# A fused matmul, bias and residual on one core: twelve deferred tiles, other load groups, and a different last-store split

## The chip, the core and the metric

The kernel runs on one core of a Trainium2 chip. The metric is device time in microseconds (us). The engines go by their short names: PE does matrix products and transposes, DVE, ACT and POOL work on elements, and SP issues the transfers (DMAs), which 16 DMA engines carry out. Most of the runs below are timed in rounds, each kernel against the kernel before on the same chip; a ratio is the mean time of one kernel's fast runs over the mean of the other's fast runs of the same rounds, so it is not quite the ratio of the medians that are quoted. The span in a profile is about 1.8 us shorter than the device time.

## The reference

```python
x:        (16, 512, 1024) float32      weight: (1024, 768) float32
bias:     (768,) float32               residual: (16, 512, 768) float32
out = matmul(x, weight) + bias + residual      # float32
```

The kernel moves 87.05 MB and does 64 tiles of 128 rows: input 33.6 MB, residual and output 25.2 MB each, weight 3.1 MB.

## The kernel before

A tile is 128 rows, one on each partition. Sixteen tiles form a stage; partition p holds 16 neighbouring rows of HBM, so a load of j tiles has one run of j rows per partition. SP issues every DMA, in the order of a list. The list has `x` (input), `w`, `b`, `r` (residual), `s` (store), `c` (last pieces of the last tile), each with stage and tiles; a fifth number of a store is the partition at which it is cut in two DMAs.

```python
EARLY_END = 14     # tiles below it are finished without the residual, which POOL adds later
TMP_ROW = 16       # their products wait in these rows of the residual and output buffer R
W_ROW = 14         # where the float32 weights land, in R as well
ADDS = [10, 14, 3, 2, 4, 15, 11, 1, 5, 13, 7, 6, 12, 9, 0, 8]
ORDER = [..., ('r', 2, 6, 16), ('s', 1, 0, 16), ('x', 3, 0, 6), ('r', 3, 0, 7), ('x', 3, 6, 16),
 ('r', 3, 7, 16), ('s', 2, 0, 16), ('s', 3, 0, 10), ('s', 3, 10, 12, 108), ('s', 3, 12, 14),
 ('s', 3, 14, 15), ('c', 3, 15, 0), ('c', 3, 15, 1)]
# ... cut ...
            elif kind == "r":        # when may a residual load be issued
                need = [("store", t - RR) for t in range(J * S + j0, J * S + j1) if t >= RR]
                # ... cut: also after the casts of weights and the adds whose rows it overwrites
# ... cut ...
                edges = [0, *cut, P]
                for p0, p1 in zip(edges, edges[1:]):
                    K_(nc.sync.dma_start(
                        out=out_d[S, p0:p1, j0:j1, n0:n0 + nl],
                        in_=R[p0:p1, (J * S + j0) % RR:(J * S + j0) % RR + j1 - j0, n0:n0 + nl],
                    ))
# ... cut ...
    def finish(t):
        p = PO[t % HEAD]
        if t < EARLY_END:            # product + bias; POOL adds the residual later
            K_(nc.vector.tensor_add(out=tmp(t), in0=p, in1=bias_sb))
        else:                        # POOL has added the bias to the residual already
            K_(nc.vector.tensor_add(out=row(t), in0=p, in1=row(t)))
# ... cut ...
    for t in range(HEAD, n_t):       # the main loop
        cast(t + 2)                  # ACT: float32 input to bfloat16
        pool_adds(t + 1)
        transp(t + 1)                # PE: four transposes, then a DVE copy
        # ... cut: 16 matmuls of tile t
        finish(t - 1)
        # ... cut
```

## Time and profile before

| | kernel before |
|---|---|
| device time, first three runs | 211.26 us median (210.89 to 211.57) |
| span of the profiled run | 209.4 us |
| last DVE add ends | 204.48 us |
| last store lands on its 16 engines | 206.18 to 208.30 us |

The landings come from the semaphore events of the trace: a store over 128 partitions has 16 of them (the last store's run from 206.18 to 208.30), read here as one for each of the 16 DMA engines, at the time when its share has landed. The store of 108 rows has 12 and that of 20 rows 10, beside one just after the issue (194.87 and 196.17) that is not counted. No view numbers the engines. The numbers 0 to 15 that the prediction and the expectations give them are labels by the rows that an engine carries, an estimate from the counts of landings: 108 rows on 12 engines are nine each, 20 on 10 are two; in the changed kernel, 100 on 10 are ten, 28 on 14 are two. The traces agree with it: eight of the ten landings of the 20-row store come 0.45 to 0.48 us after one of the 108-row store (two rows of 0.234 us), and in the changed kernel each of the ten landings of the 100-row store has one of the 28-row store 0.21 to 0.25 us after it (two rows of 0.121 us). That a label means the same engine under both cuts was assumed, not shown.

The views that carry the argument are shown in the prediction.

```profile
101.05 0.60 PE L157 MATMUL pt<-ident,xb 128*128 128x128 f32 x4
104.08 0.60 PE L157 MATMUL pt<-ident,xb 128*128 128x128 f32 x4
107.12 0.60 PE L157 MATMUL pt<-ident,xb 128*128 128x128 f32 x4
```

The middle line is tile 32, the first tile of the third stage.

### The profile page before, as it was taken

Reading aid. Unit: us, or ns where it says so; the run is one execution under the profiler, and the core shown is the slowest. Engines: PE = TensorE matmul, PEld = TensorE weight load, DVE = VectorE, ACT = ScalarE, POOL = GpSimd, SP = SyncE. Lnnn points to the kernel's source line nnn. Section 1 sums busy time; section 2 is a strip of 40 time slices with the busy share of each in tenths; the row PEclk is TensorE's granted clock in tenths of the full one; section 3 lists DMA queues with packets and bytes.
Section 4 is the critical chain, followed back from the end, with each engine's and each line's share of the span. In section 5 each row is a group of like instructions: output and inputs, shape, how many; then the busy total and the mean of one; then the engine's idle time right before and its main releaser. Section 6 shows DMA issues by size and latency. Waiting matters only on the chain.

```text
span 209.4 us, 3113 instructions
## 1 busy us (share of the span) xinstructions
PE 202.3 (97%) x1298; PEld 130.3 (62%) x1298; DVE 104.7 (50%) x140; ACT 66.1 (32%) x69; POOL 115.9 (55%) x72
## 2 busy tenths in 40 slices
PE   7999999999999999999999999999999999999990
PEld 2455666666666666666666666666666666666650
DVE  0448555445544554554455454645544554554460
ACT  2444513312730371310460083320180065330000
POOL 2100039769999806997049603999009940799200
PEclk9999999999999999999999999999999999999998
DMA  6999999999989899899999999999999999998984
GB/s 232 426 425 429 428 433 457 393 464 410 472 378 495 383 494 415 385 415 444 408 435 479 408 417 474 441 412 390 424 476 399 459 407 449 451 441 384 415 354 166
DMA packets 4780, 87.24 MB, mean 417 GB/s; under 512 B 538, under 2 KB 666, under 8 KB 1694
## 3 DMA queue, kind: packets, MB, share of 16 engines
q1 hardware_dynamic: 4766, 87.05, 97.6%
q8 instruction: 10, 0.16, 0.3%
q14 instruction: 4, 0.03, 0.0%
HBM read 61.88 MB, written 25.17 MB: 416 GB/s over the span
## 4 chain that ended last, share of the span: by engine, by line
PE 92%; DMA 4%; ACT 1%; DVE 1%; SPq 0%; issue 0%
PE psum_o L164 78%; PE pt L157 13%; DMA x_tile<-in_x_dram 4%; PE psum_o L258 1%; ACT xb L146 1%; DVE xt L158 0%; DVE ro L262 0%; SPq L119 0%; SPq L122 0%
## 5 line engine op out<-in xcount | busy, mean ns | idle before, releaser
L164 PE MATMUL psum_o<-w_sb,xt 128*128 128x512 bf16 x1008 | 174.0, 326 | 0.3 <-DVE xt L158 0.3
L164 PEld LDWEIGHTS <-xt 128*128 128x128 bf16 x1008 | 98.5, 98 | 59.0 <-DVE xt L158 0.7
L189 POOL TENSOR_TENSOR ro<-ro,bias_sb 128x768 f32<-128x768 f32 x50 | 88.9, 1822 | 48.0 <-DMA ro<-in_residual_dram 37.4
L149 ACT CAST xb<-x_tile 128x1024 bf16<-128x1024 f32 x60 | 59.7, 1043 | 113.8 <-DMA x_tile<-in_x_dram 62.7
L158 DVE COPY xt<-pt 128x1024 bf16<-128x1024 bf16 x64 | 44.0, 691 | 84.9 <-PE pt L157 84.8
L199 DVE TENSOR_TENSOR ro<-psum_o,ro 128x768 f32<-128x768 f32 x49 | 46.5, 948 | 4.3 <-POOL ro L189 3.2
L185 POOL TENSOR_TENSOR ro<-ro 128x768 f32<-128x768 f32 x14 | 25.0, 1815 | 25.1 <-DMA ro<-in_residual_dram 25.0
L157 PE MATMUL pt<-ident,xb 128*128 128x128 f32 x256 | 38.5, 274 | 0.2 <-ACT xb L146 0.2
L157 PEld LDWEIGHTS pt<-ident,xb 128*128 128x128 f32 x256 | 29.9, 142 | 9.0 <-ACT xb L146 1.1
L195 DVE TENSOR_TENSOR ro<-psum_o,bias_sb 128x768 f32<-128x768 f32 x14 | 13.2, 948 | 0.0
L208 PE MATMUL psum_o<-warm 128*128 128x512 bf16 x12 | 5.3, 632 | 1.2 <-DVE warm_a L204 1.2
L229 ACT CAST w_sb<-ro 128x768 bf16<-128x768 f32 x4 | 3.3, 832 | 3.7 <-DMA ro<-in_weight_dram 3.7
L208 PEld LDWEIGHTS <-warm 128*128 128x128 bf16 x12 | 1.6, 144 | 3.9 <-issue 2.8
L229 POOL CAST w_sb<-ro 128x768 bf16<-128x768 f32 x1 | 0.8, 822 | 5.5 <-DMA ro<-in_weight_dram 5.5
L149 DVE CAST xb<-x_tile 128x1024 bf16<-128x1024 f32 x1 | 0.7, 693 | 4.4 <-DMA x_tile<-in_x_dram 4.4
L146 ACT CAST xb<-x_tile 128x512 bf16<-128x512 f32 x3 | 1.8, 616 | 3.4 <-PE psum_o L164 1.7
L258 PE MATMUL psum_o<-w_sb,xt 128*128 128x512 bf16 (+1 forms) x16 | 2.8, 326 | 0.0
L229 DVE CAST w_sb<-ro 128x768 bf16<-128x768 f32 x3 | 1.7, 558 | 2.0 <-DMA ro<-in_weight_dram 2.0
L147 DVE CAST xb<-x_tile 128x512 bf16<-128x512 f32 x3 | 1.2, 424 | 2.4 <-DMA x_tile<-in_x_dram 2.4
L258 PEld LDWEIGHTS <-xt 128*128 128x128 bf16 x16 | 1.6, 98 | 1.1
L223 PE MATMUL psum_o<-warm 128*128 128x512 bf16 x6 | 1.6, 379 | 0.0
L262 DVE TENSOR_TENSOR ro<-psum_o,ro 128x512 f32<-128x512 f32 (+1 forms) x2 | 1.1, 558 | 0.9 <-PE psum_o L258 0.8
(14 smaller groups left out, 5.1 us busy)
## 6 DMA issues: line engine op xcount, KB each, us to landing
out_dram<-ro SPq DMA_DIRECT2D x3, 6144.0 KB, 34.1
x_tile<-in_x_dram SPq DMA_DIRECT2D x3, 5120.0 KB, 24.1
ro<-in_residual_dram SPq DMA_DIRECT2D x3, 3840.0 KB, 25.2
x_tile<-in_x_dram SPq DMA_DIRECT2D x3, 3072.0 KB, 40.2
ro<-in_residual_dram SPq DMA_DIRECT2D x3, 2304.0 KB, 17.5
x_tile<-in_x_dram SPq DMA_DIRECT2D x4, 1024.0 KB, 8.2
x_tile<-in_x_dram SPq DMA_DIRECT2D x2, 2048.0 KB, 21.0
out_dram<-ro SPq DMA_DIRECT2D x1, 3840.0 KB
```

Of the source, the lines that this page charges most:

```text
L146: K_(nc.scalar.copy(out=dst[:, 0:K // 2], in_=src[:, 0:K // 2]))
L149: K_((nc.scalar.copy if how == "s" else nc.vector.tensor_copy)(out=dst, in_=src))
L157: K_(nc.tensor.transpose(out=pt[:, q, :], in_=words[:, ts(q, P)], identity=ident))
L158: K_(nc.vector.tensor_copy(out=XT[t % XT_N].rearrange("p q m e -> p (q m e)"), in_=pt.rearrange("p q m -> p (q m)").bitcast(BF16),))
L164: K_(nc.tensor.matmul(PO[t % HEAD][:, n0:n0 + nl], lhsT=XT[t % XT_N][:, q, :, e], rhs=w_sb[:, q, e, n0:n0 + nl], start=(q == 0 and e == 0) ...
L185: K_(nc.gpsimd.tensor_add(out=r, in0=r, in1=tmp(t)))
L189: K_(nc.gpsimd.tensor_add(out=r, in0=r, in1=bias_sb))
L195: K_(nc.vector.tensor_add(out=tmp(t), in0=p, in1=bias_sb))
L199: K_(nc.vector.tensor_add(out=row(t), in0=p, in1=row(t)))
L208: K_(nc.tensor.matmul(PO[0][:, 0:512], lhsT=warm[:, 0:P], rhs=warm, start=True, stop=True))
L229: K_(copy(out=w_sb[:, q, e, :], in_=w_st[:, 2 * q + e, :]))
L258: K_(nc.tensor.matmul(p, lhsT=XT[t % XT_N][:, q, :, e], rhs=w_sb[:, q, e, n0:n0 + nl], start=(q == 0 and e == 0), stop=(q == n_q - 1 and e ...
```

## The change

Its intent: defer fewer tiles (12, not 14), load the first nine residual tiles at once, regroup the loads of the third stage (the first input load holds eleven tiles in place of six, the first residual load ten) and the stores of the first, and split the last stores differently. In place of tiles 58 and 59 (108 rows on 12 engines, 20 on 10), tile 55 is held back and stored as 100 rows on 10 engines and 28 on 14, to take work from the engines that are late at the end. The whole diff:

```diff
--- before.py
+++ after.py
@@ -18,10 +18,10 @@
 XT_N = 4
 XB_N = 4
 WARM = 12
-EARLY_END = 14
-TMP_ROW = 16
-W_ROW = 14
-ADDS = [10, 14, 3, 2, 4, 15, 11, 1, 5, 13, 7, 6, 12, 9, 0, 8]
+EARLY_END = 12
+TMP_ROW = 18
+W_ROW = 5
+ADDS = [6, 14, 3, 4, 8, 1, 15, 2, 5, 9, 13, 12, 11, 7, 0, 10]
 HEAD_ORDER = [('cast', 0, 'v'), ('cast', 1, 's'), ('tr', 0), ('tr', 1), ('wc', 0, 0, 's'), ('wc', 0, 1, 'g'),
  ('warm', 3), ('mm', 0, 0), ('mm', 1, 0), ('cast', 2, 'sv'), ('cast', 3, 'sv'), ('warm', 3),
  ('tr', 2), ('tr', 3), ('wc', 1, 0, 's'), ('wc', 1, 1, 'v'), ('mm', 2, 0), ('mm', 0, 1),
@@ -29,12 +29,12 @@
  ('mm', 2, 2), ('wc', 3, 0, 's'), ('wc', 3, 1, 'v'), ('bias',), ('cast', 4, 'sv'), ('mm', 0, 3),
  ('fin', 0), ('mm', 1, 3), ('mm', 2, 3)]
 ORDER = [('x', 0, 0, 2), ('w', 0, 0, 2), ('x', 0, 2, 4), ('w', 1, 0, 2), ('b', 0, 0, 0), ('w', 2, 0, 2),
- ('w', 3, 0, 2), ('x', 0, 4, 6), ('x', 0, 6, 10), ('r', 0, 0, 6), ('x', 0, 10, 14),
- ('r', 0, 6, 16), ('x', 0, 14, 16), ('x', 1, 0, 6), ('r', 1, 0, 6), ('x', 1, 6, 16),
- ('r', 1, 6, 16), ('s', 0, 0, 16), ('x', 2, 0, 6), ('r', 2, 0, 6), ('x', 2, 6, 16),
- ('r', 2, 6, 16), ('s', 1, 0, 16), ('x', 3, 0, 6), ('r', 3, 0, 7), ('x', 3, 6, 16),
- ('r', 3, 7, 16), ('s', 2, 0, 16), ('s', 3, 0, 10), ('s', 3, 10, 12, 108), ('s', 3, 12, 14),
- ('s', 3, 14, 15), ('c', 3, 15, 0), ('c', 3, 15, 1)]
+ ('w', 3, 0, 2), ('x', 0, 4, 6), ('x', 0, 6, 10), ('r', 0, 0, 9), ('x', 0, 10, 12),
+ ('x', 0, 12, 16), ('r', 0, 9, 16), ('x', 1, 0, 6), ('r', 1, 0, 6), ('x', 1, 6, 16),
+ ('r', 1, 6, 16), ('s', 0, 0, 10), ('x', 2, 0, 11), ('r', 2, 0, 10), ('s', 0, 10, 16),
+ ('x', 2, 11, 16), ('r', 2, 10, 16), ('s', 1, 0, 16), ('x', 3, 0, 6), ('r', 3, 0, 6),
+ ('x', 3, 6, 16), ('r', 3, 6, 16), ('s', 2, 0, 16), ('s', 3, 0, 7), ('s', 3, 8, 12),
+ ('s', 3, 7, 8, 100), ('s', 3, 12, 14), ('s', 3, 14, 15), ('c', 3, 15, 0), ('c', 3, 15, 1)]
 LAST = [(0, 512), (512, 256)]
 
 
```

## The prediction

> **What bounds the kernel now.** I read the page first (busy shares and the 40 slices), then the waits of PE alone, then the chain that ended last, then the last microseconds as a table of stages, and finally the semaphore events of the trace, which give for each DMA the landing on each of its engines.
>
> ```profile
> PE 202.3 (97%) x1298; PEld 130.3 (62%) x1298; DVE 104.7 (50%) x140; ACT 66.1 (32%) x69; POOL 115.9 (55%) x72
> ...
> PE   7999999999999999999999999999999999999990
> ...
> DMA  6999999999989899899999999999999999998984
> ...
> q1 hardware_dynamic: 4766, 87.05, 97.6%
> q8 instruction: 10, 0.16, 0.3%
> ```
>
> Two resources are full at once. PE is at nine tenths or more in every slice but the first and the last; the DMA engines are at nine tenths nearly everywhere, and their packets take 97.6% of 16 engines' span. The mean of 417 GB/s includes a start and an end without transfers.
>
> ```profile
> PE psum_o L208 <- DVE warm_a L204: 1.2, 1, 1.2
> PE psum_o L164 <- DVE xt L158: 0.3, 1, 0.3
> PE pt L157 <- ACT xb L146: 0.2, 1, 0.2
> ```
>
> That is all PE ever waits: 1.7 us, all of it before 20 us. In the chain of the whole span, the main loop is one block of 2.60 us of matmuls and 0.44 us of transposes per tile, every 3.04 us, from 22.26 us to the end. No reordering of the DMAs can shorten that part. What is left is the tail:
>
> ```profile
> 201.42 2.62 PE psum_o L258 x16
> 204.03 0.02 issue
> 204.06 0.42 DVE ro L262
> ```
>
> PE ends at 204.04, the last add at 204.48, the span at 209.4: 4.9 us are stores. In the table of stages the DMA share falls just before the last stores are issued, and is high again when they run:
>
> ```profile
> 200.00:202.00 2.00, 2.00 (x14) 1.13 (x12) 0.89 (x2) 0.00 (x0) 0.00 (x0) 1.00 0.73 270
> 202.00:204.00 2.00, 2.00 (x14) 1.08 (x12) 1.18 (x2) 0.00 (x0) 0.00 (x0) 1.00 1.01 416
> 204.00:206.00 2.00, 0.02 (x1) 0.00 (x0) 0.42 (x1) 0.00 (x0) 0.00 (x0) 1.00 0.92 365
> 206.00:208.00 2.00, 0.00 (x0) 0.00 (x0) 0.00 (x0) 0.00 (x0) 0.00 (x0) 1.00 0.25 92
> ```
>
> From 206 to 208 few engines still work (share 0.25). The semaphore events say the same: the last store (256 columns of tile 63), issued at 204.51, lands on its 16 engines from 206.18 to 208.30, the median at 206.7 and the last two at 207.9 and 208.3. So the end is set by one or two late DMA engines, about 1.5 us behind the median.
>
> [...] ten packets of 16384 bytes on the instruction queue, each 1.01 to 1.11 us long, from 23.5 to 196.0 us. Each holds up one DMA engine: the residual load of tiles 0 to 5 lands on 15 engines by 28.5 and on the sixteenth at 29.7, after the fetch at 23.5; the two fetches at 175.96 and 196.01 are still visible at the tail (below).
> [...] the store of 108 rows has 12 landings, that of 20 rows has 10; no view numbers the engines[...] the full slices here average about 427 GB/s[...].
>
> **The change part by part.**
> PE, ACT: the instruction order is the same, and so is the work; DVE and POOL run the same number of adds (two tiles change from "product plus bias, then POOL adds the residual" to "POOL adds bias, then DVE adds"; 0.948 us on DVE and 1.82 us on POOL in both forms). Worth 0. Bytes: the same 87.05 MB; two more DMAs.
> Head: the weights are staged in other rows, so the first residual load must now wait for casts of the first two weight blocks, and is issued after about 13 us, not at 7.41. The queue then still holds input tiles 4 to 9, which land at 23.0 in the kernel before, so no hole opens. Worth 0.
> Middle: I laid the DMAs of the new order end to end at the old stream's rate (6.29 MB of output in 14.5 us, 433 GB/s) and asked two things.
> (1) Does a DMA get issued before the queue runs dry? Residual 16 to 21 waits for the seventh POOL add: five adds of 1.8 us from 32.5, then tiles 8 and 2, about 45.3 (before: 40.51); input 16 to 21 occupies the queue until 52. Residual 32 to 41 waits for the landing of output 0 to 9, 80.4 + 3.93/0.434 = 89.5; input 32 to 42 fills the queue to 102.8. Residual 42 to 47 waits for output 10 to 15, about 118.9; input 43 to 47 runs to 123.6. All fit; the margins are 3 us or more.
> (2) Does data arrive in time for PE? Input 32 to 42 lands at 80.4 + (3.93 + 5.77)/0.433 = 102.8, where before it was 102.2; a cast of 1.04 makes it 103.9, and the transposes of tile 32 start at 104.3 (22.26 + 27 x 3.04). Margin 0.4 us, before 1.0. Residual 32 to 41 lands near 112.1 (before, tiles 32 to 37 at 107.7); add, DVE add and the copy queued behind it end at 115.5, and the matmuls that need them start at 116.8: margin 1.3. Residual 54 to 63 lands at 179.0 as before (same bytes ahead), but now holds tile 54, needed one tile sooner: POOL until 180.9, DVE add until 181.9, next copy until 182.6, needed at 183.6: margin 1.1. Input 54 to 63 gains, with one residual tile less ahead: 0.39 MB or 0.9 us. So PE should not stall. Worth 0, with a risk.
> Tail: here is the gain. Packet times in the trace: 0.234 us per 6144-byte row, 0.121 per 3072, 0.084 per 2048, 0.046 per 1024. Relative to eight rows on each engine (16 engines), the split of tiles 58 and 59 into 108 and 20 rows costs engines 0 to 9 three rows more, +0.70; engines 10 and 11 one row more, +0.23; engines 12 to 15 save all eight, -1.87. The new split of tile 55 (one tile, 3072-byte rows): engines 0 to 9 carry 12 rows, +0.48; 10 to 13 carry two, -0.73; 14 and 15 none, -0.97.
> Who is late before? The store of tiles 48 to 57 lands on the engines at 199.3 to 201.4, and on two at 202.4 and 202.55. The latest (202.55) plus nine rows, 2.1, gives 204.6, which is the last landing of the 108-row store; the 20-row store's last is 204.07, so this engine is not among 0 to 9: it is engine 10 or 11. It then needs 8 x (0.234 + 0.121 + 0.084 + 0.046) = 3.88 and would land at 208.5; the trace says 208.30. The second late one at the end is an engine of 0 to 9: 201.4 + 2.57 + 3.88 = 207.85 (trace 207.9). The one at 202.4 is among 12 to 15, relieved: 206.3.
> After: engine 10 or 11: 208.3 - 0.23 - 0.73 = 207.3. Engines 0 to 9: 207.9 - 0.70 + 0.48 = 207.7. The one among 12 to 15: 202.4 + 0.95 (one full tile more ahead of it than the ten counted before) + 0.24 or 0 (two rows or none of tile 55) + 3.88 = 207.5 or 207.2. The last is 207.7 in place of 208.3: 0.6 us less. The unused time at 200 to 202 (engines 12 to 15 done too early, waiting for tile 60) shrinks as well, worth 0.1 on the mean, inside the same 0.6.
> Sum: 0 + 0 + 0 - 0.6: 211.26 - 0.6 = 210.7.
>
> **The rivals.**
> (a) A PE stall takes the gain back. For: the margin of 0.4 us at tile 32 is less than the lag that one more late engine makes (1.2 us), and POOL's releases move later. Against: the last landing of 102.2 already contains lags of that kind. PE cannot catch up, so a stall of 0.5 to 0.8 us moves the last add by as much, though part hides behind the late engines: 210.7 to 211.5.
> (b) The relief goes to the wrong engines. If the fetches hit the engines in another order with the new timing, a late engine among 0 to 9 (202.5 + 0.95 + 1.45 + 3.88) lands at 208.8, 0.5 worse: 211.8. [...]
> (c) The tail closes fully: no engine can be done before the last store's own latency, 204.51 + 1.67 = 206.18 at the earliest, and 206.7 at the old median. If all engines met there, 1.6 us less: 209.7. Against: the fetches at 176 and 196 remain.
> (d) A hole in the DMA stream from SP's in-order queue (it stood up to 33.3 us on one wait before). One of 2 us would go fully to the end, 212.7; my margins are against it.
>
> **The range and the chances.** The three times before spread 0.7 us. (a) and (b) reach 211.5 to 211.8, (c) 209.7; I take 210.0 to 211.6 as eight in ten. Two per cent is 4.2 us. Faster by that is not to be had: even with no late engine the tail holds 1.6 us. Slower would need a stall or hole of several microseconds. So 0.01 faster, 0.97 within, 0.02 slower.
>
> **What would show it.** Right: PE's waits stay at 1.7 us, PE ends near 204.0, the last landing spreads less than 2.1 us over its engines and ends near 207.7, and the span is near 208.8. Wrong: a PE wait on an input cast near 104 us or on a DVE copy near 115 or 183 us (rival a), a last landing past 208.3 with PE unmoved (b), or a DMA share well under nine tenths in the middle (d).

## The result, and the profile after

| | before | changed |
|---|---|---|
| device time, six runs each | 211.01 us (210.64 to 211.57) | 211.25 us (210.93 to 211.46) |
| ratio, 95% interval | | 1.0008 (0.9991 to 1.0024) |
| span of the profiled run | 209.4 | 209.3 |
| last DVE add ends | 204.48 | 205.17 |
| last store lands: first, median, last engine | 206.2, 206.7, 208.30 | 206.9, 207.0, 208.28 |

The time is the same. The 0.6 us that were forecast are not there. From the page of the changed kernel, the parts shown of the kernel before:

```profile
PE 201.2 (96%) x1273; PEld 130.4 (62%) x1298; DVE 104.7 (50%) x140; ACT 66.5 (32%) x69; POOL 115.8 (55%) x72
...
DMA  6999999999999899999999999999999999998994
...
q1 hardware_dynamic: 5056, 87.05, 97.8%
q8 instruction: 10, 0.16, 0.3%
```

The DMA stream is as full as before, with no hole. (PE shows 25 fewer matmuls because the trace lost some records; the program has the same number.) The waits of PE, in the same columns as before (us in total, times, longest):

```profile
PE psum_o L208 <- DVE warm_a L204: 1.2, 1, 1.2
PE pt L157 <- ACT xb L149: 0.5, 1, 0.5
PE psum_o L164 <- DVE xt L158: 0.3, 1, 0.3
PE pt L157 <- ACT xb L146: 0.2, 1, 0.2
```

The second line is new. The chain that ended last shows where it is (start, length, what):

```profile
76.07 27.45 DMA x_tile<-in_x_dram
...
103.62 1.05 ACT xb L149
...
104.71 0.66 PE pt L157 x4
```

The eleven-tile input load lands at 103.52, the cast of tile 32 ends at 104.67, and tile 32's transposes start at 104.71, where they stood at 104.08 before. Below, a stall at tile 32 is the time by which these transposes start later than 3.04 us after the ones before them: 0.69 us here. (The list of waits counts 0.5: ordinarily the transposes start 0.16 us before the matmuls ahead of them are shown to end.) PE never makes that up. At the end, the chain:

```profile
202.11 2.61 PE psum_o L258 x16
204.72 0.02 issue
204.75 0.42 DVE ro L262
```

PE is done 0.69 us later than before (204.72 against 204.03), yet the last landing is the same: 208.28 against 208.30. The table of stages of the tail (length, then PE, PEld, DVE, ACT and POOL busy, clock, then DMA share and GB/s):

```profile
200.00:202.00 2.00, 2.00 (x15) 1.23 (x13) 1.10 (x2) 0.00 (x0) 0.00 (x0) 1.00 0.84 343
202.00:204.00 2.00, 2.00 (x13) 1.02 (x11) 1.02 (x2) 0.00 (x0) 0.00 (x0) 1.00 0.98 396
204.00:206.00 2.00, 0.71 (x7) 0.39 (x4) 1.06 (x2) 0.00 (x0) 0.00 (x0) 1.00 0.86 344
206.00:208.00 2.00, 0.00 (x0) 0.00 (x0) 0.00 (x0) 0.00 (x0) 0.00 (x0) 1.00 0.43 158
```

The DMA share from 200 to 202 has risen (0.84 against 0.73), and from 206 to 208 more engines work than before (0.43 against 0.25): the tail is better filled, but its last stores are issued later and it ends at the same time.

Two readings fit this. Theory S: the tail gained its 0.6 us and the stall at tile 32 took it back. Theory L: the stall is hidden, because one late DMA engine is busy without a pause to the end, and this engine was later by itself. Evidence for L: the last four stores land last at 206.40, 207.33, 207.94 and 208.28: steps of 0.93, 0.61 and 0.34 us, close to the eight packets of 0.121, 0.084 and 0.046 us that each store puts on an engine. That engine did not wait for PE.

### The profile page after: what moved, and what is told of

Its sections match the earlier page's. It is cut to its first block, busy times and chain, and to the rows that moved or that the text cites. A ratio compares the mean times of both kernels' runs of the same rounds, so it can differ in the third digit from the quotient of the medians.

```text
span 209.3 us, 3091 instructions
## 1 busy us (share of the span) xinstructions
PE 201.2 (96%) x1273; PEld 130.4 (62%) x1298; DVE 104.7 (50%) x140; ACT 66.5 (32%) x69; POOL 115.8 (55%) x72
## 4 chain that ended last, share of the span: by engine, by line
PE 76%; DMA 17%; ACT 2%; issue 2%; DVE 1%; SPq 0%; ACTq 0%
PE psum_o L164 64%; DMA x_tile<-in_x_dram 17%; PE pt L157 11%; ACT xb L149 2%; PE psum_o L258 1%; DVE xt L158 0%; ACT xb L146 0%; DVE ro L262 0%; SPq L119 0%; SPq L122 0%; ACTq L149 0%
## 5 line engine op out<-in xcount | busy, mean ns | idle before, releaser
L164 PE MATMUL psum_o<-w_sb,xt 128*128 128x256 bf16 (+1 forms) x983 | 172.7, 324 | 1.6 <-DVE xt L158 0.3
L189 POOL TENSOR_TENSOR ro<-ro,bias_sb 128x768 f32<-128x768 f32 x52 | 92.4, 1818 | 51.8 <-DMA ro<-in_residual_dram 51.8
L199 DVE TENSOR_TENSOR ro<-psum_o,ro 128x768 f32<-128x768 f32 x51 | 48.4, 950 | 11.9 <-POOL ro L189 10.8
L185 POOL TENSOR_TENSOR ro<-ro 128x768 f32<-128x768 f32 x12 | 21.4, 1818 | 24.2 <-DVE xt L158 24.2
L195 DVE TENSOR_TENSOR ro<-psum_o,bias_sb 128x768 f32<-128x768 f32 x12 | 11.3, 948 | 0.0
```

Of the source, the lines that this page charges most:

```text
L164: K_(nc.tensor.matmul(PO[t % HEAD][:, n0:n0 + nl], lhsT=XT[t % XT_N][:, q, :, e], rhs=w_sb[:, q, e, n0:n0 + nl], start=(q == 0 and e == 0) ...
L185: K_(nc.gpsimd.tensor_add(out=r, in0=r, in1=tmp(t)))
L189: K_(nc.gpsimd.tensor_add(out=r, in0=r, in1=bias_sb))
```

## The experiments

All kernels compute the correct result except the one that says otherwise. A table of their traces first; the text after it says what each tells. "Late engine ahead" is the last landing of the store of tiles 32 to 47: how far behind the latest engine is when the tail starts.

| run | time, median | ratio to before (95%) | last add ends | late engine ahead | last store: first, median, last | span |
|---|---|---|---|---|---|---|
| before, first trace | 211.01 | | 204.48 | 193.50 | 206.2, 206.7, 208.30 | 209.4 |
| before, again | 210.69 | 1.0005 (0.9992 to 1.0018) | 204.51 | 193.71 | 206.5, 206.7, 208.04 | 209.1 |
| changed, first | 211.25 | 1.0008 (0.9991 to 1.0024) | 205.17 | 194.36 | 206.9, 207.0, 208.28 | 209.3 |
| changed, second | 211.21 | 1.0014 (0.9997 to 1.0032) | 204.80 | 193.98 | 206.5, 206.8, 208.47 | 209.5 |
| changed, third | 210.67 | 1.0004 (0.9991 to 1.0016) | 204.59 | 193.56 | 206.3, 206.6, 207.58 | 208.6 |
| new tail alone | 210.88 | 0.9996 (0.9980 to 1.0012) | 204.65 | 194.11 | 206.3, 206.5, 208.02 | 209.1 |
| changed, old tail | 210.93 | 1.0003 (0.9984 to 1.0022) | 204.93 | 194.54 | 206.6, 206.8, 208.00 | 209.1 |
| changed, load split | 210.99 | 1.0006 (0.9989 to 1.0022) | 204.73 | 194.28 | 206.6, 206.8, 208.20 | 209.2 |
| changed, 6 more matmuls | 211.12 | 1.0025 (1.0011 to 1.0039) | 206.11 | 194.11 | 207.8, 207.9, 208.03 | 209.1 |
| changed, 18 more | 213.26 | 1.0122 (1.0108 to 1.0136) | 208.64 | 193.47 | 210.4, 210.4, 210.53 | 211.5 |
| changed, two stores less | 209.49 | 0.9946 (0.9933 to 0.9958) | 204.72 | 192.13 | 206.4, 206.5, 206.59 | 207.6 |
| before, even rows | 211.34 | 1.0033 (1.0021 to 1.0046) | 204.51 | 193.53 | 206.2, 206.3, 208.12 | 209.1 |
| changed, even rows | 211.50 | 1.0038 (1.0025 to 1.0052) | 204.70 | 193.59 | 206.4, 206.5, 208.46 | 209.6 |
| changed, four more tiles cut | 215.00 | 1.0206 (1.0192 to 1.0220) | 204.90 | 194.47 | 209.7, 209.8, 212.48 | 213.4 |

Each set of runs shared one chip and its rounds of the kernel before: first, the changed kernel's second run, the new tail alone, the old tail and the split load; second, six more matmuls, two stores less, even rows in the old tail and the kernel before again; third, the other four. Across sets only the ratios compare.

### The changed kernel again

No edit.

> The changed kernel once more, for a second trace and for its time in the same rounds as the three below. Both theories: ratio 0.998 to 1.003 to the kernel before. Theory S (the PE stall of 0.7 us at tile 32 took the gain of the tail back): the stall is there again, 0.4 to 0.9 us. Theory L (one late DMA engine, busy without a pause to the end, sets the end, whatever PE does): the last store's last landing again trails its median by 1.2 us or more.

It held: ratio 1.0014, the stall is there but smaller (0.4 us, at the low end of what S expected: the eleven-tile load landed at 103.15, not 103.52), and the last landing trails its median by 1.7 us.

### The new tail alone

```diff
 kernel before
- ('s', 3, 0, 10), ('s', 3, 10, 12, 108), ('s', 3, 12, 14),
+ ('s', 3, 0, 7), ('s', 3, 8, 12), ('s', 3, 7, 8, 100), ('s', 3, 12, 14),
```

> The kernel before with the new order and split of the last stores alone. The middle is the old one, so PE must not stall at tile 32 and its last add should end near 204.5. Theory S: the full gain of the prediction shows, last landing near 207.7, time 0.4 to 0.6 us under the kernel before (ratio 0.997 to 0.998). Theory L: the late engine decides; if it is as late as in the first trace of the kernel before the gain is the same 0.6 us, if as late as in the changed kernel's trace there is none (ratio 0.999 to 1.001).

Ratio 0.9996: no gain of 0.6 us (0.997) without the stall either. The middle is the old one and PE is held up at tile 32 by only 0.13 us (its transposes start at 104.00), and once more by as much at tile 54, so theory S has little to blame. The late engine ended the store of tiles 32 to 47 at 194.11, later than in the kernel before (193.50), although the program up to there is the same: the lateness is not fixed by the program. Nor is it by the chip: three later runs shared one chip and the same program up to that store, and there it was 193.56, 193.59 and 194.47.

### The changed kernel with the old tail

```diff
 changed kernel
- ('s', 3, 0, 7), ('s', 3, 8, 12), ('s', 3, 7, 8, 100), ('s', 3, 12, 14),
+ ('s', 3, 0, 10), ('s', 3, 10, 12, 108), ('s', 3, 12, 14),
```

> The changed kernel with the old last stores (tiles 48 to 57 at once, tiles 58 and 59 as 108 and 20 rows): the change of head and middle alone. Theory S: the stall of 0.7 us stays and nothing pays for it, 0.4 to 0.7 us slower than the kernel before (ratio 1.002 to 1.0035). Theory L: the new middle leaves the late engine about 0.8 us later, and the old tail gives it 0.96 us less relief than the new one: 0.6 to 1.0 us slower (ratio 1.003 to 1.005), with the last landing near 209.

Both theories missed: 1.0003, not 1.002 or more (the interval, to 1.0022, just touches the least that S expected). The stall at tile 32 was 0.55 us and cost nothing that can be seen. Lateness explains why L missed: the latest engine ended the store of tiles 48 to 57 at 203.56, but neither the store of 108 rows (last landing 203.83) nor that of 20 rows (204.30) has a landing 2.1 us after that, as nine rows would take. So here the latest engine was one of those that the old cut spares, while in the first trace of the kernel before it was one that carries nine rows (204.61).

### The eleven-tile load split

```diff
 changed kernel
- ('x', 2, 0, 11),
+ ('x', 2, 0, 6), ('x', 2, 6, 11),
```

> The changed kernel with the input load of tiles 32 to 42 issued as two loads, 32 to 37 and 38 to 42, in the same place of the queue. The bytes ahead of tile 32 fall by 5 tiles, so it lands near 97, and the stall at tile 32 must go (PE waits 1.7 us, last add ends near 204.5). Theory S: 0.4 to 0.7 us faster than the changed kernel, ratio 0.997 to 0.998 to the kernel before. Theory L: the late engine is busy to the end either way, so no change beyond 0.2 us, ratio 1.000 to 1.002.

The first part lands at 97.23 and tile 32's transposes start at 103.95, without a stall:

```profile
100.92 0.60 PE L157 MATMUL pt<-ident,xb 128*128 128x128 f32 x4
103.95 0.60 PE L157 MATMUL pt<-ident,xb 128*128 128x128 f32 x4
```

The stall's cause is thereby shown: eleven tiles land as one. But the time is 1.0006 against the changed kernel's 1.0014 in the same rounds, a difference (0.17 us) inside both intervals, and the last landing is 208.20. L expected such a ratio, but this run does not decide between the theories: PE stalled elsewhere, 0.33 us at tile 48, whose input load landed at 151.67. So the last add ended at 204.73, not near 204.5 as expected, and only 0.07 us sooner than in the changed kernel's second trace (204.80). The runs with more matmuls and with fewer stores, below, decide.

### Six more matmuls

```diff
 changed kernel, main loop
+            if t == 40:
+                for _ in range(6):
+                    mm_extra(t)        # into the bank that the real matmuls then overwrite
```

> The changed kernel with six needless 512-column matmuls ahead of tile 40's, 6 x 0.217 = 1.3 us of PE time that nothing can catch up. Theory S (PE's time sets the end): 1.0 to 1.3 us slower than the changed kernel, about 212.3. Theory L (a late DMA engine, busy to the end, sets it, and PE has slack of 1.5 us before it): the last add moves by about 1.3 us, the last landing by less than 0.4, time within 0.4 us of the changed kernel, about 211.3 to 211.6.

The chain ends, and the tail's stages read:

```profile
205.66 0.02 issue
205.69 0.42 DVE ro L271
```

```profile
204.00:206.00 2.00, 1.65 (x12) 0.94 (x10) 1.12 (x3) 0.00 (x0) 0.00 (x0) 1.00 0.93 373
206.00:208.00 2.00, 0.00 (x0) 0.00 (x0) 0.11 (x1) 0.00 (x0) 0.00 (x0) 1.00 0.60 217
```

PE ends 0.9 us later than even in the first trace of the changed kernel, and the last store still lands at 208.03. Now all sixteen engines land within 0.22 us (207.81 to 208.03), where the first had been done 1.4 us before the last (206.86 to 208.28). The time is 1.0025, that is 0.2 to 0.4 us over the three ratios of the changed kernel (1.0004 to 1.0014), for 1.3 us of work (an estimate: 0.217 us for each matmul, from the 2.60 us of a tile's 16, eight of 512 columns and eight of 256). S expected 1.0 to 1.3 and is refuted.

### Two stores less (a wrong result)

```diff
 changed kernel, in the store of tiles 10 to 15
+                if (S, j0) == (0, 10):
+                    j1 -= 2            # tiles 14 and 15 are never written
                # ... cut: j1 is restored after the DMA
```

> The changed kernel without the stores of tiles 14 and 15 (128 x 2 rows of the output stay unwritten: a wrong result on purpose), 0.79 MB or 1.84 us less of DMA stream at 427 GB/s. Theory S: the last add stays near 204.7 to 205.2 and so does the time, within 0.3 us of the changed kernel. Theory L: the late engine is done 1.8 us sooner, and the end comes 1.0 to 1.6 us earlier, until the store latency of about 1.7 us after the last issue becomes the limit: time 209.6 to 210.2.

Ratio 0.9946: with the changed kernel at 1.0004 to 1.0014, taking 1.84 us off the DMA stream (estimated, 0.79 MB at 427 GB/s) saves 1.2 to 1.4 us, as L expected (the median, 209.49, is a little under the 209.6 to 210.2 written down, as the kernel before also ran at 210.64 here). PE's end did not move out of its range:

```profile
204.27 0.02 issue
204.30 0.42 DVE ro L266
```

```profile
204.00:206.00 2.00, 0.26 (x3) 0.00 (x0) 0.61 (x2) 0.00 (x0) 0.00 (x0) 1.00 0.78 296
206.00:208.00 2.00, 0.00 (x0) 0.00 (x0) 0.00 (x0) 0.00 (x0) 0.00 (x0) 0.79 0.08 25
```

All engines land within 0.15 us (206.44 to 206.59) and the span is the last add plus 2.9 us (204.72 to 207.6). This is what the end looks like when PE sets it.

### Eighteen more matmuls

The same edit with `range(18)`.

> The changed kernel with 18 needless matmuls, 18 x 0.217 = 3.9 us of PE time, where 6 of them (1.3 us) cost 0.1 to 0.3 us. If the late engine leaves PE a slack of about 1.3 us and the end then follows the last add by 3.0 us, the span is 206.1 + 2.6 + 3.0 = 211.7 and the time about 213.3 to 213.7, ratio 1.012 to 1.015. If PE had more slack than that, less.

Ratio 1.0122, 213.26 us: the ratio as computed, the time a hair under the range. Again the landings are close together (210.35 to 210.53) and the span, 211.5, is the last add, 208.64, plus 2.9. So the two limits can be put in numbers: the span is the later of the last add plus 2.9 us and the last landing of the late engine plus 1.0 to 1.1 us. For the changed kernel's third trace the first is 207.5 and the second 208.6: PE had 1.1 us to spare.

### Even rows in the old tail

```diff
 kernel before
- ('s', 3, 10, 12, 108),
+ ('s', 3, 10, 12),
```

> The kernel before with the store of tiles 58 and 59 over all 128 rows, so without any relief of the high-numbered engines. By the prediction's own sum on the first trace the late engine among 10 and 11 gains 0.23 and the one at 202.4 among 12 to 15 loses 1.87: last landing 202.55 + 1.87 + 3.88 = 208.3, no change, ratio 0.999 to 1.001. If the cut is worth what its engines save, 0.5 to 1 us slower (1.0025 to 1.005).

Ratio 1.0033, 0.7 us slower: the old cut is worth that much. My own sum, applied to the first trace, says that the cut is worth nothing, and is wrong. The traced execution, at 209.1 us of span, was the fastest of its five (the others 209.5 to 209.9), so this trace cannot be used for the size.

### Even rows in the new tail

```diff
 changed kernel
- ('s', 3, 7, 8, 100),
+ ('s', 3, 7, 8),
```

> The changed kernel with tile 55 stored over all 128 rows at its place behind tiles 56 to 59. Theory L with the cut aimed right: the late engine, if among 10 to 15, carries 0.73 to 0.97 us more, so 0.4 to 0.7 us slower than the changed kernel, ratio 1.003 to 1.005 to the kernel before, as the even rows were for the old tail. If the new cut gives relief to engines that are not late, no change beyond 0.2 us.

Ratio 1.0038 where the changed kernel had 1.0004 in the same rounds: also 0.7 us. The late engine lands at 204.77 with its eight rows of tile 55 and at 208.46 at the end, while the median engine is done at 206.5. So the new cut works, and is worth the same as the old one.

### The changed kernel a third time

> The changed kernel a third time, in the rounds of the three below: 0.999 to 1.0025 of the kernel before. Its trace again shows a last landing between 207.9 and 208.6, on an engine that need not be the same as before.

1.0004, and the trace refutes the expected range for the landing (207.9 to 208.6): its last landing is 207.58. Here the late engine left the store of tiles 32 to 47 at 193.56, as in the first trace of the kernel before, there was no stall at tile 32, and the end came out within 0.1 us of the 207.7 that the prediction had worked out from that lateness. PE's chain at tile 32 in this execution:

```profile
101.30 0.44 PE pt L157 x4
...
104.33 0.46 PE pt L157 x4
```

### The kernel before again

> The kernel before, unchanged, timed against itself: ratio 0.9985 to 1.0015. For its second trace. If the lateness is a fixed pattern, the store of 108 rows lands last at 204.6, that of 20 rows at 204.1 and the last store at 208.3, all within 0.2 us, as in the first trace. If which engine is late, and by how much, changes from execution to execution, these move by 0.3 us or more and in different directions.

Ratio 1.0005, so the rounds are sound. The trace differs from the first: the store of 108 rows lands last at 203.76 (first trace 204.61), that of 20 rows at 204.26 (204.07), the last store at 208.04 (208.30). They moved in different directions, so another set of engines was late.

### Four more tiles cut

```diff
 changed kernel
- ('s', 3, 8, 12), ('s', 3, 7, 8, 100),
+ ('s', 3, 8, 12, 100), ('s', 3, 7, 8, 100),
```

> The changed kernel with tiles 56 to 59 also stored as 100 and 28 rows: engines 0 to 9 carry 12 rows of 12288 bytes in place of 8, 4 x 0.46 = 1.84 us more, and become the late ones. By the arithmetic of rows and packet times the last landing is 209.4 to 210.2 and the time 1.2 to 1.8 us over the changed kernel, ratio 1.007 to 1.010. If rows per engine do not decide, no change beyond 0.3 us.

Ratio 1.0206: the sign is as expected and the size is more than twice the expected. Rows per engine decide, but they were not all that changed:

```profile
200.00:202.00 2.00, 2.00 (x14) 1.22 (x13) 0.89 (x2) 0.00 (x0) 0.00 (x0) 1.00 0.74 237
202.00:204.00 2.00, 2.00 (x14) 1.12 (x12) 1.23 (x2) 0.00 (x0) 0.00 (x0) 1.00 0.98 270
204.00:206.00 2.00, 0.45 (x5) 0.15 (x2) 0.80 (x2) 0.00 (x0) 0.00 (x0) 1.00 0.82 232
```

From 202 to 204 us the engines are as busy as in the changed kernel (0.98) but move 270 GB/s in place of 396. The packets of 12288 bytes took 626 ns on the mean and up to 1.9 us, where the changed kernel's took 464 and at most 0.69; the median is 460 in both, and 26 of the 128 took over 600 ns. The store of 28 rows landed last at 207.09, 2.9 us after that of 100 rows (204.16), where its two packets of 460 ns on an engine would take 0.9. My sum had used the packet time of even stores. Why these packets are slower is not shown. With one tile of 3072-byte rows (the change itself) the effect is small: all packets of that size in the tail took 124 ns on the mean, median 121.

## Why the prediction was right, and where it was wrong

The measured 211.25 lies in the range of 210.0 to 211.6, and "within 2%" was right. But the range also holds no change at all (211.26), so that it was met says nothing for the gain. The expected gain of 0.6 us was not there. By its steps:

**What bounds the kernel.** Right that both PE and the DMA stream are full (slices 2 to 36 average 432 GB/s, not the 427 that it gives) and that the tail is set by the last one or two DMA engines. The six extra matmuls and the two missing stores show it.

**Head, 0.** Right. The first residual load was issued at 13.13 and the DMA slices that follow stay at nine tenths.

**Middle, no hole.** Right. Residual 16 to 21 was issued at 44.97 (predicted 45.3), residual 32 to 41 at 90.16 (89.5), residual 42 to 47 at 118.15 (118.9), and of the slices between the start and 188 us one is at eight tenths, where there were three.

**Middle, data in time.** The size was off by tenths where the margin was tenths. The eleven-tile load landed at 103.52, 103.15 and 102.94 in the three traces (predicted 102.8, margin 0.4 us before tile 32), so PE stalled in two of three. Residual 32 to 41 landed at 112.3 to 112.7 (112.1; the sum that was meant, 102.8 + 3.93/0.433, gives 111.9), residual 54 to 63 at 179.3 to 180.1 (179.0; its margin was 183.6 - 182.6 = 1.0, not 1.1), both without a wait of PE. Rival (a) came true as a stall and failed as a cost: PE had more than a microsecond of slack.

**Tail, 0.6 us less.** This step failed, in the sentence "The last is 207.7 in place of 208.3". It is the term that was mis-sized: the new tail alone measured 0.9996, from 0.4 us faster to 0.3 us slower. Three things in it:

1. It started from one execution, and by later measure a long one. The first trace has a span of 209.4. It lies in the middle of its own six runs (211.16 us among 210.64 to 211.57), but of 34 later executions of the kernel before, on three chips, two reached that span; their median is 208.9.
2. It took the lateness of each engine in that one execution as fixed. The second trace of the kernel before has other late engines; there the two latest (202.8 after tile 57) are among the engines that the old cut spares, as no landing of the 108-row store comes 2.1 us later, and the end is set by an engine with eleven rows. By the same sum that engine gains 0.70 - 0.48 = 0.22 us from the new cut (208.04 to 207.8) and the two latest come to 202.8 + 0.95 + 0.24 + 3.88 = 207.9 at most, so the gain would have been 0.1 to 0.2 us. In the old-tail run the latest engine was one that the old cut spares.
3. It therefore missed what the old cut was already worth. The sum says that even rows would have changed nothing (208.3 against 208.3); measured, even rows cost 0.33%. The new cut is worth 0.34% (1.0038 against 1.0004). The change swaps one cut for another of the same value, which is where the expected gain went.

Rival (b), the relief going to the wrong engines with a changed order, is the nearest to what happened, with one correction: I counted on the fetches (the packets of 16384 bytes on the instruction queue, 0.88 to 1.11 us each in the first traces of the two kernels) coming at unchanged times. The traces contradict that: there are ten in every trace of these kernels, but the eighth starts at 157.3, 159.3 and 157.1 us in the three traces of the changed kernel, and at 156.6 and 158.0 in the two of the kernel before. Which engines end up late does not stay the same either. The trace does not number the engines, so that it is the fetches that make other engines late each time is argued, not shown. The first trace of the kernel before shows as much: after the fetch at 23.54 one engine lands late (29.67, the other fifteen by 28.45), after the second, at 40.70, two do (43.69 and 43.83, the other fourteen by 42.45).

**Left open.** The last landing ahead of the tail is 193.50 to 194.11 in four traces with the old middle (mean 193.7) and 193.47 to 194.54 in nine with the new one (mean 194.0, the run with fewer stores left out). Whether the new middle makes the late engine later, or the chips and executions differed, can't be told from these.

None of the correct versions beats the kernel before: the best, the new tail alone at 0.9996, is not to be told from it.

## What to carry to other kernels

When compute and DMA are both full, find out which of them sets the end before working on either: add a known amount of work to the one, take a known amount from the other, and look at how far apart the engines' last landings are (in these traces 1.3 to 2.8 us where a late DMA engine set the end, 0.2 us where the compute side did). A stall of the compute engine costs nothing while it is shorter than the slack that a late engine leaves (1.1 us in one trace here), and a gain worked out engine by engine from one trace should be worked out again on a second trace of the same kernel, and tested on what the sum says of the code that is already there. An uneven last store was worth 0.3% here; pushed further, it came with slower packets (626 ns in place of 464 for 12288 bytes).
